# A transformer layer's step order: attention units, projections, modulation tiles and parts of the recurrence are named one by one, and some are moved

## The chip, the cores and the metric

The kernel runs on one core of a Trainium2 chip. The core has a matrix engine (TensorE, PE in the profile, with its weight loads as PEld), a vector engine (VectorE, DVE), a scalar engine (ScalarE, ACT), a general engine (GpSimd, POOL) and a queue processor that issues nearly all DMAs here (SyncE, SP). Each engine takes its instructions in one fixed order; semaphores tie them together. The metric is the device time of one execution in microseconds (us). Three runs of the kernel before took 1702.09, 1701.49 and 1700.19 us: the median is 1701.49 us.

## The reference

One layer of a streaming encoder, for 1024 prompt frames of one stream and 64 new frames of another (with a cache of 256 past frames), model width 1024, all in fp32:

```
mod = silu(c) @ w_ada + b_ada                 # 6 vectors: shift, scale, gate, twice
h   = rms_norm(x) * (1 + sc1) + sh1
proj = h @ w_in                               # one projection for both head groups
# 8 RWKV-7 heads of 64: r, k, v, decay, a, g from proj (token shift, small up-projections)
s = s*w - (s@kk)(kk*a) + v k ;  y = s @ r     # per frame, per head: 64 x 64 state
y = (group_norm(y) + bonus) * sigmoid(dg) @ w_gate_up
# 8 forgetting-attention heads of 64: QK-norm, cumulative log-forget bias, causal softmax
mix = concat(y_rwkv, y_fox) @ w_out
x = x + gt1 * mix
h2 = rms_norm(x) * (1 + sc2) + sh2
x = x + gt2 * ((silu(h2 @ w_gate) * (h2 @ w_up)) @ w_down)
```

Outputs are x, the recurrent states, the shift rows, and keys, values and log-forget values of the attention heads.

## The kernel before

**Matrix products.** fp32 accuracy is had from operands that are split in a high and a low part (`split`, L212 on ACT for the high part, L216 on DVE for the low one). `mm3` (L291 to L296) makes three matmuls for each block of 128 rows: high weights by high data (L294), high by low (L295), low by high (L296). A weight block of 128x1024 comes by DMA into the ring `wraw` (four buffers), its parts into `whi` and `wlo` (two buffers each).

**Stages.** The tokens are worked on in two halves: half 0 has 512 prompt frames, half 1 the other 512 and the 64 new ones. In the order of the trace: a start, in which the first 16 of 40 modulation tiles are made and `h` with them (to about 35 us); the phase of half 0 (to about 340 us) and of half 1 (to about 720 us), with the projections, the RWKV heads and the preparation of attention; attention of half 0 (about 665 to 744 us); attention of half 1 with the output projection of half 0 between its heads (about 744 to 905 us); output projection of half 1 and the second norm; the feed-forward part (to about 1430 us) and its down projection to the end.

**What sets the order.** The program emits steps one after another, and a list scheduler then orders the instructions of each engine. It works on the emission order with dependencies and buffers known, so neighbouring steps are interleaved, but a step that is emitted much later is not pulled far forward. Three things set the emission order:

- `ORDER` (L35, L36), a string of tokens for each half that `phase` reads. D, Z, A, B, N are an RWKV head pair's decay part, its three projections (k, r and v, with the square of k), its preparation, its chain over chunks of 64 frames, and its normalisation with the gate; T and U do a chain and a normalisation that half 0 left over; Q, K, q, k, V, C, L, O, S, P belong to attention's inputs, the log-forget values and the statistics.
- `proj` (L298): before it loads a projection's weights it takes one modulation tile off the list `background` and does it whole. There are 24 of these. Such a tile (`ada_mm`, L181 to L193, and `ada_fin`, L195 to L201) is a load `wada` into the ring `wraw`, 16 matmuls into `pada` with 32 columns of the array each, a copy `mrow` on ACT (L193), a transpose on PE (`pada<-ident,mrow`, L198) and a sum `mred` on DVE (L200).
- `Pipe(2)` in `run` (L1461, L1483). `attend` gives a head's units (two query blocks of 256 in half 0, three in half 1). A unit is a generator with stops: scores `psc` (L910, L912, mask L916), row maximum `nm` on DVE (L920), exponential `p` on ACT (L922) and scaling; then transposes `ppt` (L940) whose results are split to `pth` (ACT, L953) and `ptl` (DVE, L954); then `pav` (L962) and the output `fy` (DVE, L969). `Pipe` keeps two units under way and steps them in turn.

For half 1's attention the program calls `residual_x` (loads of x into `x1_0`, L996) and then `load_mix` of half 0 after head 0. `load_mix` brings eight blocks of mixed heads back from memory (`mixt<-yscr`, L984, two buffers): the first four are RWKV output (split to `mixrh`, `mixrl`), the others attention output that half 0's attention has stored from `fy` (L974, split to `mixfh`, `mixfl`). After each head but the first one tile of the output projection is done (`outproj`, result `po`, by `mm3`; its evacuation is on DVE, L1002). Since half 1's attention has other PSUM pools on the same banks, its first scores wait for the last `fy` of half 0.

Of the kernel before, what the change touches and what calls it, by code (L numbers as in the profile page):

```python
# [10 lines left out]
AF = mybir.ActivationFunctionType  # L11
# [5 lines left out]
P = 128  # L17
D = 1024
# [16 lines left out]
ORDER = ("Z0 D0 A0 D1 Z1 L Q0 B0 V0 N0 A1 C0 Z2 D2 q0 O A2 K0 k0 B1 K1 V2 Z3 D3 Q1 q1 V1 C1 A3 S k1 Q2 N1 q2 Q3 B2 N2 K2 k2 V3 K3 k3 C2 q3 C3",  # L35
         "Z0 T3 L D0 A0 Z1 U3 D1 B0 Q0 A1 D2 K0 Z2 A2 k0 D3 Q1 q0 N0 B1 K1 k1 q1 Z3 A3 N1 V0 V1 B2 V2 Q2 N2 q2 K3 Q3 q3 P B3 K2 k3 k2 V3")  # L36
# [28 lines left out]
class K:  # L65
# [351 lines left out]
    def rwkv_a(self, hf, j, z, d):  # L417

        nc, vc, O = self.nc, self.vc, self.O
# [4 lines left out]
        zk, zr, zv, sq = z  # L424
# [22 lines left out]
        for h in range(2):  # L447
# [6 lines left out]
            bon[:, off:off + m], ps, zv[:, off:off + m], op=ALU.mult), "ra")  # L454

        At = self.rpool.tile([P, 9, 2, 2, 64], F32, tag="At", name="At")
        for c in range(0, nch, 4):
            m = min(4, nch - c)

            pa = [self.ps([P, 4, P], tag="ra", name="pA") for _ in range(2)]  # L460
            for i in range(m):
                for h in range(2):
                    hp = slice(64 * h, 64 * h + 64)
                    nc.tensor.matmul(pa[h][:, i], kb[hp, c + i], rk[hp, c + i], start=True, stop=True)  # L464
            for h in range(2):
                nc.vector.tensor_tensor(At[:, c:c + m, :, h], pa[h][:, 0:m].rearrange("p i (x t) -> p i x t", x=2),
                                        self.amask[:, h:h + 1].rearrange("p o (x t) -> p o x t", x=2)
                                        .to_broadcast([P, m, 2, 64]), op=ALU.mult)

# [30 lines left out]
    def rwkv_b(self, hf, j, st):  # L500
# [14 lines left out]

        def small(name, blocks, mm):
# [20 lines left out]
        for h in range(2):  # L537
            for x in range(2):
                r = 64 * h + 32 * x
                nc.scalar.copy(inv[r:r + 16, 0:nch, r + 16:r + 32], pg[h][r:r + 16, 0:nch, 16:32])  # L540

# [16 lines left out]
        nc.gpsimd.memset(rk[64:128, 0:nch, 0:64], 0.0)  # L558

# [9 lines left out]
        for t0 in range(0, nch, 8):  # L569
# [6 lines left out]
            for x in range(min(2, m)):  # L576
                for h in range(2):
                    nc.scalar.copy(sv[64 - 64 * h:128 - 64 * h, t0 + x:t0 + m:2, h],
                                   pt[64 * x:64 * x + 64, 0:(m - x + 1) // 2, 64 * h:64 * h + 64])

# [8 lines left out]
        for c in range(nch):  # L589
            if c == 8:  # L590
# [385 lines left out]


# [310 lines left out]
    def phase(self, hf, order, late):  # L1288
# [13 lines left out]
        d, z, st, y, y0, f = {}, {}, {}, {}, {}, {}  # L1302
        for t in order:
            op, j = t[0], int(t[1]) if len(t) > 1 else 0
            if op == "D":
                d[j] = self.rwkv_d(hf, j, zl)
            elif op == "Z":
                zk = self.proj_z(hf, 4 + j)
                sq = self.slot(name="sq", tag="sa")
                nc.scalar.activation(sq[:, 0:hf.n], zk[:, 0:hf.n], AF.Square, scale=self.vc[:, V_KK + j:V_KK + j + 1])  # L1310
                z[j] = zk, self.proj_z(hf, j), self.proj_z(hf, 8 + j), sq
            elif op == "A":
                st[j] = self.rwkv_a(hf, j, z.pop(j), d.pop(j))
            elif op == "B":
                y[j] = self.rwkv_b(hf, j, st.pop(j))
            elif op == "N":
                self.rwkv_n(hf, j, y.pop(j), zg)
            elif op == "T":
                y0[j] = late[j][0]()
            elif op == "U":  # L1320
                late.pop(j)[1](y0.pop(j))
            elif op == "L":
                self.logf(hf)
            elif op == "O":
                self.ones_rows()
            elif op in "QK":
                f[t] = self.fox_qk(hf, j, int(op == "K"))
            elif op in "qk":
                self.fox_norm(hf, j, int(op == "k"), f.pop(t.upper()))
            elif op == "V":  # L1330
                self.fox_v(hf, j)
            elif op == "C":
                self.cache_kv(j)
            elif op == "P":
                self.early()
            elif op == "S":
                self.rs1 = self.x_stat1()
        r = {j: (lambda j=j, s=s: self.rwkv_b(hf, j, s), lambda p, j=j: self.rwkv_n(hf, j, p, zg)) for j, s in st.items()}
        for j, p in y.items():
            r[j] = (lambda p=p: p, lambda p, j=j: self.rwkv_n(hf, j, p, zg))  # L1340
        return r

    def run(self):
        tc, nc, A, O = self.tc, self.nc, self.A, self.O
        halves = [Half(0), Half(1)]
        with ExitStack() as top:
# [104 lines left out]
            for b, f in late.values():  # L1451
                f(b())
# [8 lines left out]
            pipe = Pipe(2)  # L1461
            for hd in range(8):
                pipe.run(self.attend(hd, halves[0]))
            pipe.flush()
# [18 lines left out]
            pipe = Pipe(2)  # L1483
            for hd in range(8):
# [8 lines left out]
            pipe.flush()  # L1493
            self.outproj(halves[0], 7)
# [114 lines left out]
class Pipe:  # L1609


    def __init__(self, skew):
        self.skew, self.live = skew, []

    def run(self, units):
        for u in units:
            self.live.insert(0, u)
            self.step(self.skew)

    def step(self, keep):  # L1620
        self.live = [u for u in self.live if next(u, None) is not None]
        while len(self.live) > keep:
            u = self.live.pop()
            for _ in u:
                pass

    def flush(self):
        while self.live:
            self.step(len(self.live))


# [91 lines left out]
```

## Time and profile before

| what | value |
|---|---|
| runs | 1702.09, 1701.49, 1700.19 us; median 1701.49 |
| the profiled execution's own time | 1699.15 us |
| its span, first to last instruction | 1697.5 us |
| busy in the span | PE 97%, PEld 85%, DVE 66%, ACT 43%, POOL 11% |
| mean granted clock of PE | 0.992 |

The difference between the profiled execution's time and its span, 1.65 us, lies around the instructions and no order changes it. The profiled execution was 2.34 us below the median of the runs. In the page's lines a name left of `<-` is what an instruction writes, those right of it what it reads; a bracket with a releaser gives the idle time of the engine just before the instruction and what ended it. In a table of windows the columns after the stretch are its length, then the busy time of PE, PEld, DVE, ACT and POOL with the number of instructions, the granted PE clock as a share of full speed, the share of the DMA engines and GB/s.

### The profile page before, as it was taken

Reading aid. Unit: us, or ns where it says so; the run is one execution under the profiler, and the core shown is the slowest. Engines: PE = TensorE matmul, PEld = TensorE weight load, DVE = VectorE, ACT = ScalarE, POOL = GpSimd, SP = SyncE. Lnnn points to the kernel's source line nnn. Section 1 sums busy time; section 2 is a strip of 40 time slices with the busy share of each in tenths; the row PEclk is TensorE's granted clock in tenths of the full one; section 3 lists DMA queues with packets and bytes.
Section 4 is the critical chain, followed back from the end, with each engine's and each line's share of the span. In section 5 each row is a group of like instructions: output and inputs, shape, how many; then the busy total and the mean of one; then the engine's idle time right before and its main releaser. Section 6 shows DMA issues by size and latency. Waiting matters only on the chain.

```text
span 1697.5 us, 33265 instructions
## 1 busy us (share of the span) xinstructions
PE 1645.3 (97%) x12897; PEld 1439.1 (85%) x12897; DVE 1124.8 (66%) x2573; ACT 726.5 (43%) x1530; POOL 183.1 (11%) x412
## 2 busy tenths in 40 slices
PE   6999999999999999989999999999999999999999
PEld 3776776788888888767889899999999999999998
DVE  6776676757867655877877975555555556545545
ACT  4535364653545346766776633333333333211210
POOL 2102230222121213201120000000000000000000
PEclk9999999999999999989999999999999999999999
DMA  8544447541233344566654432222222215323313
GB/s 308 164 128 133 141 135 200 176 123 33 71 85 85 87 135 113 149 190 179 169 181 167 157 127 77 77 77 77 77 77 77 77 65 196 134 79 97 97 40 121
DMA packets 133580, 207.08 MB, mean 122 GB/s; under 512 B 62126, under 2 KB 70350, under 8 KB 133422
## 3 DMA queue, kind: packets, MB, share of 16 engines
q1 hardware_dynamic: 133422, 204.95, 39.5%
q8 instruction: 102, 1.67, 0.4%
q14 instruction: 56, 0.46, 0.1%
HBM read 157.65 MB, written 47.25 MB: 121 GB/s over the span
## 4 chain that ended last, share of the span: by engine, by line
PE 84%; DVE 6%; ACT 4%; DMA 3%; issue 2%; SPq 0%; POOL 0%; ACTq 0%; DVEq 0%; POOLq 0%
PE pd L1275 15%; PE pfe L1160 8%; PE pfc L1160 7%; PE pfa L1160 7%; PE pmm L294 5%; PE pmm L295 5%; PE pmm L296 5%; PE pfb L1160 4%; PE pbs L375 2%; PE pav L962 2%; PE po L294 2%; PE ppt L940 2%; PE po L296 2%; PE po L295 2%; PE pA L464 2%
## 5 line engine op out<-in xcount | busy, mean ns | idle before, releaser
L294 PE MATMUL pmm<-hhi,whi 128*128 128x288 f32 (+1 forms) x624 | 218.8, 351 | 2.3 <-ACT pb L317 1.4
L295 PE MATMUL pmm<-hlo,whi 128*128 128x288 f32 (+1 forms) x624 | 217.0, 348 | 0.0
L296 PE MATMUL pmm<-hhi,wlo 128*128 128x288 f32 (+1 forms) x624 | 215.2, 345 | 0.6 <-DVE wlo L216 0.6
L212 ACT CAST whi<-wraw 128x1024 fp32r<-128x1024 f32 (+2 forms) x116 | 99.2, 855 | 212.5 <-PE pd L1275 167.0
L1275 PE MATMUL pd<-ah,wlo 128*128 128x512 f32 (+1 forms) x528 | 173.5, 329 | 0.0
L1275 PE MATMUL pd<-al,whi 128*128 128x512 f32 (+1 forms) x528 | 173.3, 328 | 0.0
L1275 PE MATMUL pd<-ah,whi 128*128 128x512 f32 (+1 forms) x528 | 173.1, 328 | 0.0
L1279 DVE SCALAR_TENSOR_TENSOR x1t<-pd,mod,x1t 128x512 f32<-128x512 f32 x192 | 91.4, 498 | 111.5 <-PE pd L1275 111.0
L294 PEld LDWEIGHTS pmm<-hhi,whi 128*128 128x128 f32 x624 | 119.0, 191 | 14.1 <-ACT pb L317 2.0
L296 PEld LDWEIGHTS pmm<-hhi,wlo 128*128 128x128 f32 x624 | 118.7, 190 | 10.9 <-issue 1.7
L295 PEld LDWEIGHTS pmm<-hlo,whi 128*128 128x128 f32 x624 | 118.7, 190 | 9.9 <-issue 1.2
L216 DVE TENSOR_TENSOR wlo<-wraw,whi 128x1024 fp32r<-128x1024 f32 (+2 forms) x108 | 104.2, 965 | 18.8 <-ACT whi L212 18.3
L1275 PEld LDWEIGHTS pd<-al,whi 128*128 128x128 f32 x528 | 99.4, 188 | 7.7
L1275 PEld LDWEIGHTS pd<-ah,whi 128*128 128x128 f32 x528 | 99.3, 188 | 7.7
L1275 PEld LDWEIGHTS pd<-ah,wlo 128*128 128x128 f32 x528 | 99.3, 188 | 7.5
L1160 PE MATMUL pfc<-hh,hS 128*128 128x256 f32 (+1 forms) x352 | 101.6, 289 | 1.6 <-ACT hh L1062 1.6
L1160 PE MATMUL pfc<-hl,hS 128*128 128x256 f32 (+1 forms) x352 | 101.9, 289 | 0.0
L1160 PE MATMUL pfa<-hh,whi 128*128 128x256 f32 (+1 forms) x352 | 101.9, 290 | 0.0
L1160 PE MATMUL pfa<-hl,whi 128*128 128x256 f32 (+1 forms) x352 | 101.8, 289 | 0.0
L1160 PE MATMUL pfc<-hh,lS 128*128 128x256 f32 (+1 forms) x352 | 101.5, 288 | 0.0
L1160 PE MATMUL pfa<-hh,wlo 128*128 128x256 f32 (+1 forms) x352 | 101.4, 289 | 0.0
L604 POOL TENSOR_SCALAR sd<-sv,pc 64x64 f32<-64x64 f32 x136 | 76.3, 561 | 181.2 <-DVE sv L617 157.6
(361 smaller groups left out, 4383.5 us busy)
## 6 DMA issues: line engine op xcount, KB each, us to landing
wraw<-in_w_in_dram SPq DMA_DIRECT2D x52, 512.0 KB
wada<-in_w_ada_dram SPq DMA_DIRECT2D x48, 512.0 KB
as<-actscr SPq DMA_DIRECT2D x22, 544.0 KB
wraw<-in_w_gate_dram SPq DMA_DIRECT2D x22, 512.0 KB
wraw<-in_w_up_dram SPq DMA_DIRECT2D x22, 512.0 KB
wraw<-in_w_down_dram SPq DMA_DIRECT2D x40, 256.0 KB
wraw<-in_w_out_dram SPq DMA_DIRECT2D x16, 512.0 KB
actscr<-sg SPq DMA_DIRECT2D x22, 288.0 KB
```

What stands on the lines that cost most here:

```text
L212: nc.scalar.copy(hi, src)
L216: eng.tensor_tensor(lo, src, hi.bitcast(F32), op=ALU.subtract)
L294: nc.tensor.matmul(ps[0:M, 0:n], whi[:, k, 0:M], xhi[:, k, off:off + n], start=(k == 0), stop=False)
L295: nc.tensor.matmul(ps[0:M, 0:n], whi[:, k, 0:M], xlo[:, k, off:off + n], start=False, stop=False)
L296: nc.tensor.matmul(ps[0:M, 0:n], wlo[:, k, 0:M], xhi[:, k, off:off + n], start=False, stop=(k == kt - 1))
L375: nc.tensor.matmul(ps[:, 0:n], w, x[:, off:off + n], start=True, stop=True)
L464: nc.tensor.matmul(pa[h][:, i], kb[hp, c + i], rk[hp, c + i], start=True, stop=True)
L604: nc.gpsimd.tensor_scalar(sd[hsl[h]], sv[hsl[h], c, h], pc[hsl[h], c], None, op0=ALU.mult)
L940: nc.tensor.transpose(pt[0:rows, b - b0, t * P:t * P + qn], p[0:qn, pc:pc + rows], self.ident[0:qn, 0:qn])
L1160: nc.tensor.matmul(ps, l[:, k], r[:, s, k], start=(first and k == 0 and y == 0), stop=(k == 3 and y == 2), skip_group_check=True)
L1275: nc.tensor.matmul(ps[:, 0:n], w[:, i], x[:, t:t + n], start=(i == 0 and y == 0), stop=(i == len(fs) - 1 and y == 2))
L1279: nc.vector.scalar_tensor_tensor(dst, ps[:, so - off:so - off + l], self.mod[:, 40 + o, b:b + 1], dst, op0=ALU.mult, op1=ALU.add)
```

## The change

The strings get finer tokens and some tokens stand elsewhere. Z is cut into X (k and its square), Y (r) and W (v). G does one modulation tile, which `proj` no longer does. A and B become generators, and a token with `*n` advances one by n stops. `Pipe` is gone; a table `ATT` tells for each half which unit advances at each step (a number advances that unit by one stop, H starts a head's loads, R is `residual_x`, M and N are `load_mix` of half 0 and half 1, O is one tile of the output projection). M is now the first token of half 1's attention, ahead of the first head's loads; R follows the first steps of units 0 and 1; O0 comes after unit 3's steps.

```diff
-ORDER = ("Z0 D0 A0 D1 Z1 L Q0 B0 V0 N0 A1 C0 Z2 D2 ...
+ORDER = ("W0 X0 G Y0 G D0 A0*2 G A0 D1 G X1 G Y1 G W1 L G Q0 B0*12 G V0 N0 A1*3 C0 G X2 ...
...
+       "M H0 0 1 0 R 2 1 0 H1 3 2 1 4 3 2 5 4 3 O0 H2 6 5 4 7 6 5 8 6 7 O1 H3 9 8 7 10 9 8 11 10 9 O2 H4 12 11 10 13 "
+       "14 12 11 13 12 O3 H5 15 14 13 16 15 14 17 16 15 O4 N H6 17 18 16 19 18 20 17 19 18 O5 H7 21 21 20 19 22 21 "
+       "20 23 O7 22 O6 23 22 23")
...
         else:
-            if self.background:
-                self.background.pop(0)()
             whi, wlo = self.load_w(self.A["w_in"][col // P], [P, KT, P])
...
+    def att_phase(self, hf, order, more):
+        units = {}
+        for t in order:
+            if t[0] == "H":
+                us = self.attend(int(t[1:]), hf)
+                units.update({int(t[1:]) * len(us) + i: u for i, u in enumerate(us)})
+            elif t.isdigit():
+                next(units[int(t)], None)
+            else:
+                more[t[0]](int(t[1:] or 0))
...
+                elif op == "G":
+                    self.background.pop(0)()
...
-            pipe = Pipe(2)
-            for hd in range(8):
-                pipe.run(self.attend(hd, halves[1]))
-                if hd == 0:
-                    self.residual_x(halves[0])
-                    self.load_mix(halves[0])
-                if hd:
-                    self.outproj(halves[0], hd - 1)
-                if hd == 5:
-                    self.load_mix(halves[1])
-            pipe.flush()
-            self.outproj(halves[0], 7)
+            self.att_phase(halves[1], ATT[1].split(), {
+                "R": lambda j: self.residual_x(halves[0]), "M": lambda j: self.load_mix(halves[0]),
+                "N": lambda j: self.load_mix(halves[1]), "O": lambda j: self.outproj(halves[0], j)})
```

The number and kind of instructions on each engine are the same. Their order differs in three places only: at the start of half 0's phase (about 34 to 125 us of the trace before), around the turn from half 0's attention to half 1's (about 725 to 800 us), and among the later heads of half 1 (about 800 to 955 us). The three pieces below are the ones that the prediction speaks of; line numbers in the rows of the change are those of the changed kernel, where `mm3` is at L306 to L308.

**SP, the DMA queue, at the turn.** Before, the loads of the mixed heads stand behind the stores and the residual's loads:

```order
L974 DMA yscr0_71<-fy_9046 128x512
L873 DMA q2x0_9558<-qx_73 4x576
L874 DMA k2x0_9560<-kx_74 4x1344
L876 DMA vsx0_9561<-vscr0_103 128x1280
L877 DMA vsx0_9561<-vscr0_103 64x128
L996 DMA x1_0_9536<-in_x0_dram 128x1024 x2
L974 DMA yscr0_71<-fy_9258 128x512
L996 DMA x1_0_9536<-in_x0_dram 128x1024 x2
L984 DMA mixt_9745<-yscr0_71 128x512
L984 DMA mixt_9749<-yscr0_71 128x512
```

With the change:

```order
L889 DMA k1x0_9559<-kx_74 64x1344
L1015 DMA mixt_9583<-yscr0_71 128x512
L1015 DMA mixt_9587<-yscr0_71 128x512
L665 DMA yscr1_72<-y_8242 128x576
L892 DMA q2x0_9558<-qx_73 64x576
L898 DMA vsx1_8034<-vscr7_110 128x512
L893 DMA k2x0_9560<-kx_74 64x1344
L993 DMA yscr0_71<-fy_9046 128x512
L1015 DMA mixt_9591<-yscr0_71 128x512
```

The first two mixed blocks are now asked for ahead of the store of `y`, thirteen rows earlier, and the next ones between the stores and the first head's loads.

**PE at the end of half 0's attention.** Here `pav_9491` is the last product of half 0 and `psc_9593` the first score of half 1. Before:

```order
L940 MATMUL ppt_9462<-ident_130,p_9434 128x128
L940 MATMUL ppt_9471<-ident_130,p_9434 128x128 x2
L962 MATMUL pav_9491<-pth_9463,vsx1_8034 128x256
L962 MATMUL pav_9491<-ptl_9464,vsx1_8034 128x256
...
L962 MATMUL pav_9491<-pth_9472,vsx1_8034 128x256
L962 MATMUL pav_9491<-ptl_9473,vsx1_8034 128x256
...
L910 MATMUL psc_9593<-k1x0_9559,qsx0_9557 128x512
```

With the change, from the last transposes on:

```order
L959 MATMUL ppt_9479<-ident_130,p_9434 128x128 x2
L307 MATMUL po_9983<-mixrl0_9544,whi_9979 128x512
L308 MATMUL po_9983<-mixrh0_9540,wlo_9980 128x512
L306 MATMUL po_9983<-mixrh0_9540,whi_9979 128x512
L981 MATMUL pav_9491<-pth_9471,vsx1_8034 128x256
L307 MATMUL po_9983<-mixrl0_9544,whi_9979 128x512
L308 MATMUL po_9983<-mixrh0_9540,wlo_9980 128x512
L981 MATMUL pav_9491<-ptl_9472,vsx1_8034 128x256
...
L306 MATMUL po_9983<-mixrh0_9540,whi_9979 128x512
L307 MATMUL po_9983<-mixrl0_9544,whi_9979 128x512
L308 MATMUL po_9983<-mixrh0_9540,wlo_9980 128x512
L929 MATMUL psc_9625<-k1x0_9559,qsx0_9557 128x512
```

Twelve matmuls of the first output tile, four blocks of the RWKV half of `mix`, now stand among the last products of half 0 and before the first score of half 1. On DVE and ACT their splits (four of `mixrh`, four of `mixrl`) move to the same place.

**PE near the start.** Before, a modulation tile and its transpose stand on both sides of a projection's matmuls:

```order
L402 MATMUL plora_955<-xl_776,wlo1_660 128x512
L190 MATMUL pada_1099<-wada_1097,ct_141 32x128 x8
L294 MATMUL pmm_1120<-hhi_175,whi_1116 128x512
L375 MATMUL pbs_975<-sq_840,bones_634 128x512
L295 MATMUL pmm_1120<-hlo_176,whi_1116 128x512
L296 MATMUL pmm_1120<-hhi_175,wlo_1117 128x512
L198 MATMUL pada_1099<-ident_130,mrow_1108 128x128
```

With the change, three of them meet between two projections:

```order
L202 MATMUL pada_920<-wada_918,ct_141 32x128 x8
L409 MATMUL plora_938<-xl_776,whi1_658 128x512
L412 MATMUL plora_937<-xl_776,wlo0_659 128x512
L412 MATMUL plora_938<-xl_776,wlo1_660 128x512
L202 MATMUL pada_1008<-wada_1006,ct_141 32x128
L210 MATMUL pada_920<-ident_130,mrow_929 128x128
L202 MATMUL pada_1008<-wada_1006,ct_141 32x128 x7
L210 MATMUL pada_1008<-ident_130,mrow_1017 128x128
L202 MATMUL pada_1098<-wada_1096,ct_141 32x128 x8
L210 MATMUL pada_1098<-ident_130,mrow_1107 128x128
L385 MATMUL pbs_958<-sq_861,bones_634 128x512
L306 MATMUL pmm_1120<-hhi_175,whi_1116 128x512
```

In return the projections ahead of it, W0 and X0, follow the ones made at the start with no modulation tile between them.

More of the change, by code (lines that the diff above doesn't have):

```diff
@@ L454, in rwkv_a @@
             bon[:, off:off + m], ps, zv[:, off:off + m], op=ALU.mult), "ra")
+        yield
         At = self.rpool.tile([P, 9, 2, 2, 64], F32, tag="At", name="At")
@@ L468, in rwkv_a @@
                                         .to_broadcast([P, m, 2, 64]), op=ALU.mult)
+        yield
         nb = 2 * ng
@@ L514, in rwkv_b @@
                 nc.sync.dma_start(inv[r, 0:nch, r], du[g, x].rearrange("g s t -> s g t"))
+        yield
         def small(name, blocks, mm):
@@ L558, in rwkv_b @@
         nc.gpsimd.memset(rk[64:128, 0:nch, 0:64], 0.0)
+        yield
         kbt = kb
@@ L579, in rwkv_b @@
                                    pt[64 * x:64 * x + 64, 0:(m - x + 1) // 2, 64 * h:64 * h + 64])
+        yield
         hsl = [slice(0, 64), slice(64, 128)]
@@ L589, in rwkv_b @@
         for c in range(nch):
+            if c:
+                yield
             if c == 8:
@@ L1301, in phase, with step @@
         self.sigm(zg[:, 0:hf.n], 1.0)
-        d, z, st, y, y0, f = {}, {}, {}, {}, {}, {}
+        d, z, f, gen = {}, {}, {}, {}
+        st, y = {}, {}
+        def step(key, make, done, j):
+            if key not in gen:
+                gen[key] = make()
+            try:
+                next(gen[key])
+            except StopIteration as e:
+                done[j] = e.value
+        y0 = {}
         for t in order:
+            t, _, times = t.partition("*")
             op, j = t[0], int(t[1]) if len(t) > 1 else 0
[L1305 to L1341, printed above, removed]
+            for _ in range(int(times or 1)):
+                if op == "D":
+                    d[j] = self.rwkv_d(hf, j, zl)
+                elif op == "X":
+                    zk = self.proj_z(hf, 4 + j)
+                    sq = self.slot(name="sq", tag="sa")
+                    nc.scalar.activation(sq[:, 0:hf.n], zk[:, 0:hf.n], AF.Square, scale=self.vc[:, V_KK + j:V_KK + j + 1])
+                    z[j, 0], z[j, 3] = zk, sq
+                elif op == "Y":
+                    z[j, 1] = self.proj_z(hf, j)
+                elif op == "W":
+                    z[j, 2] = self.proj_z(hf, 8 + j)
+                elif op == "G":
+                    self.background.pop(0)()
+                elif op == "A":
+                    step(t, lambda: self.rwkv_a(hf, j, [z.pop((j, i)) for i in range(4)], d.pop(j)), st, j)
+                elif op == "B":
+                    step(t, lambda: self.rwkv_b(hf, j, st.pop(j)), y, j)
+                elif op == "N":
+                    self.rwkv_n(hf, j, y.pop(j), zg)
+                elif op == "T":
+                    step(t, late[j][0], y0, j)
+                elif op == "U":
+                    late.pop(j)[1](y0.pop(j))
+                elif op == "L":
+                    self.logf(hf)
+                elif op == "O":
+                    self.ones_rows()
+                elif op in "QK":
+                    f[t] = self.fox_qk(hf, j, int(op == "K"))
+                elif op in "qk":
+                    self.fox_norm(hf, j, int(op == "k"), f.pop(t.upper()))
+                elif op == "V":
+                    self.fox_v(hf, j)
+                elif op == "C":
+                    self.cache_kv(j)
+                elif op == "P":
+                    self.early()
+                elif op == "S":
+                    self.rs1 = self.x_stat1()
@@ L1343, in run @@
+        return {j: (lambda j=j, s=s: self.rwkv_b(hf, j, s), lambda p, j=j: self.rwkv_n(hf, j, p, zg)) for j, s in st.items()} | {
+            j: (lambda: iter(()), lambda p, j=j: self.rwkv_n(hf, j, p, zg), p) for j, p in y.items()}
     def run(self):
@@ L1450, in run @@
             hst.close()
-            for b, f in late.values():
-                f(b())
+            for _, f, p in late.values():
+                f(p)
             nc.sync.dma_start(O["shift"], self.ns)
@@ L1460, in run @@
             self.att_pools(att, R)
-            pipe = Pipe(2)
-            for hd in range(8):
-                pipe.run(self.attend(hd, halves[0]))
-            pipe.flush()
+            self.att_phase(halves[0], ATT[0].split(), {})
             at0.close()
@@ L1606, in run @@
             self.down(halves, pre, x1t, lambda g, f: self.act_load(f, apools[g % 2]))
[L1609 to L1629, printed above, removed]
 class Rows:
```

12 lines of the change are left out of this document (7 added, 5 removed), and 1 row of the table ATT.

## The prediction

> **What bounds the kernel now.** I read the page's head first, then the chain of waits, then windows of the region that the change touches, and last PE's own timeline there.
>
> ```profile
> span 1697.5 us, 33265 instructions
> ...
> PE 1645.3 (97%) x12897; PEld 1439.1 (85%) x12897; DVE 1124.8 (66%) x2573; ACT 726.5 (43%) x1530; POOL 183.1 (11%) x412
> ...
> PE 84%; DVE 6%; ACT 4%; DMA 3%; issue 2%; SPq 0%; POOL 0%; ACTq 0%; DVEq 0%; POOLq 0%
> ```
>
> PE is the bound, with 97% of the span busy and 84% of the chain that ended last. No instruction is added or removed, so the change can only fill PE's holes, open new ones, or alter the clock at which PE's work runs. The whole of PE's idle time is 1697.5 - 1645.3 = 52.2 us, and that is spread over everything; the order is untouched outside three places. So the question is how much is lost there. The windows around the turn from half 0's attention to half 1's:
>
> ```profile
> 725.00:740.00 15.00, 11.39 (x66) 7.92 (x66) 13.44 (x38) 10.44 (x32) 1.71 (x11) 1.00 0.65 196
> 740.00:755.00 15.00, 12.92 (x45) 9.61 (x45) 7.89 (x15) 6.93 (x15) 0.41 (x2) 0.55 0.72 218
> 755.00:780.00 25.00, 22.77 (x121) 16.65 (x122) 19.75 (x39) 16.75 (x35) 3.01 (x5) 1.00 0.65 185
> 780.00:830.00 50.00, 49.22 (x307) 40.00 (x306) 39.90 (x85) 34.69 (x80) 5.85 (x14) 1.00 0.58 147
> 880.00:930.00 50.00, 50.00 (x338) 45.74 (x337) 37.79 (x64) 32.46 (x55) 2.14 (x5) 1.00 0.43 149
> ```
>
> Three things are to be seen. In the first stretch PE idles 3.61 of 15 us while DVE is busy 13.44: DVE sets the pace of half 0's last units. In the second PE looks busy (12.92), but the granted clock is 0.55: it works at half rate. In the third it idles 2.23 us at full clock. Later, from 780 us on, there is next to nothing left to fill (0.78 us, then 0.00). PE's idle time in the first three is 7.92 us together.
>
> PE's timeline tells which waits these are:
>
> ```profile
> 738.69 0.33 PE L940 MATMUL ppt<-ident,p 128*128 128x128 f32 x1 [1.02 <-DVE p L928]
> ...
> 741.12 0.39 PE L962 MATMUL pav<-pth,vsx 128*128 128x256 f32 x1 [0.46 <-ACT pth L953]
> 741.85 0.58 PE L962 MATMUL pav<-ptl,vsx 128*128 128x256 f32 x1 [0.34 <-DVE ptl L954]
> ...
> 744.68 0.80 PE L910 MATMUL psc<-k1x,qsx 128*128 128x512 f32 x1 [0.97 <-DVE fy L969]
> ```
>
> The last unit of half 0 goes from engine to engine with nothing beside it: transposes, split, product, evacuation, and only then half 1's first scores. 1.02 + 0.46 + 0.34 + 0.97 = 2.79 us are lost so.
>
> **Part 1: filler at the turn.** The first mixed blocks wait on SP in the order of the program, not for data:
>
> ```profile
> 730.19 0.94 SPq L874 DMA_DIRECT2D k2x<-kx  x1
> ...
> 744.66 0.33 SPq L974 DMA_DIRECT2D yscr<-fy  x1
> 745.03 0.92 SPq L996 DMA_DIRECT2D x<-in_x_dram  x2
> 746.00 0.90 SPq L984 DMA_DIRECT2D mixt<-yscr  x2
> ```
>
> The store `yscr<-fy` at 744.66 holds SP until half 0's last `fy`, and `mixt` stands behind it. With the change the first two `mixt` stand thirteen rows earlier, ahead of the store of `y`, so they go out before 730 us. One pair of their splits and the rate of the matmuls are in these rows (tile views of `mixrl` and `mixrh`, timeline of PE):
>
> ```profile
> L216 DVE TENSOR_TENSOR mixrl<-mixt,mixrh x4: 664/674/683, 756.5 to 763.0; 128x512 fp32r<-128x512 f32 x4
> ...
> L212 ACT CAST mixrh<-mixt x8: 616/648/675, 754.7 to 847.7; 128x512 fp32r<-128x512 f32 x4, 128x576 fp32r<-128x576 f32 x4
> ...
> 757.47 0.39 PE L295 MATMUL po<-mixrl,whi 128*128 128x512 f32 x1
> 757.70 0.39 PE L296 MATMUL po<-mixrh,wlo 128*128 128x512 f32 x1
> 757.93 0.39 PE L294 MATMUL po<-mixrh,whi 128*128 128x512 f32 x1
> ```
>
> A `po` follows the one before after 0.23 us, so twelve of them are 2.76 us of PE work that comes to stand in the 2.79 us of holes. Against it: four `mixrl` at 0.67 us are 2.7 us more on DVE, which in the first stretch has only 15 - 13.44 = 1.56 us free; three of them stand before half 0's last split. What is behind them on DVE is the `ptl` and `fy` for which PE waits. The bounds are a gain of 2.8 us (all filled, DVE's added work fits in its own waits) and a loss of 1 us (2.7 less 1.56, with the fillers waiting too). I take +1.5 us, since the last `fy` itself waited while DVE had nothing to do after 742.8 us.
>
> **Part 2: the half clock.** Windows of one stretch at a time:
>
> ```profile
> 742.00:755.00 13.00, 11.72 (x39) 8.84 (x39) 6.57 (x13) 5.70 (x12) 0.41 (x2) 0.50 0.74 213
> 755.00:756.00 1.00, 1.00 (x9) 1.00 (x9) 1.00 (x2) 1.00 (x3) 0.00 (x0) 0.97 0.37 91
> ...
> 738.20:741.60 3.40, 2.36 (x12) 1.53 (x12) 2.53 (x8) 2.15 (x6) 0.00 (x0) 0.97 0.72 276
> ...
> 277.00:278.00 1.00, 1.00 (x3) 0.80 (x4) 0.88 (x3) 0.26 (x1) 0.00 (x0) 0.59 0.80 262
> ...
> 280.00:281.00 1.00, 1.00 (x4) 0.64 (x3) 1.00 (x2) 0.04 (x1) 0.00 (x0) 0.70 0.98 272
> ```
>
> The clock falls right after a 3.4 us stretch in which PE was busy 2.36 us, and comes back at about 755. An earlier fall began at 277.4 and ended at 280.7 us (0.59 and 0.70 of a us at the mean say so). 11.72 us of PE work at half rate are 5.86 us at full rate, so 5.9 us is the most that can be won. With up to 2.76 us of dense matmuls in the stretch that brought the clock down, and the next fillers (`po<-mixfh`) between half 1's first scores, I expect that it mostly stays up. Bounds 0 and 5.9; I take 4.5 us, because an early return is worth most of it as well.
>
> [...]
>
> **Part 3: the rest of the turn.** At 766.90, 771.11 and 771.84 PE waited 0.68, 0.50 and 0.23 us:
>
> ```profile
> 766.90 0.30 PE L962 MATMUL pav<-pth,vsx 128*128 128x64 f32 x1 [0.68 <-DVE fy L969]
> ...
> 771.11 0.50 PE L294 MATMUL po<-mixfh,whi 128*128 128x512 f32 x1 [0.50 <-ACT mixfh L212]
> 771.84 0.50 PE L295 MATMUL po<-mixfl,whi 128*128 128x512 f32 x1 [0.23 <-DVE mixfl L216]
> ```
>
> The attention blocks of `mix` come too late for `po` because the `mixt` share two buffers and stand between the second head's loads on SP. With the change all eight stand ahead of the second head's loads. Bounds 0 and the 2.23 us of the stretch; I take 1.2 us. In the later heads (780 us and on) nothing can be won, and heads 3 and 4 lose their filler between scores; with PE idle 0.00 to 0.78 us in 50 I take 0, with bounds of 2 us lost and 1 us won.
>
> **Part 4: modulation tiles near the start.** Here the change opens holes. The nearest rows:
>
> ```profile
> 32.06 0.47 PE L198 MATMUL pada<-ident,mrow 128*128 128x128 f32 x1 [1.13 <-ACT mrow L193]
> ...
> 48.15 0.65 PE L190 MATMUL pada<-wada,ct 128*32 128x128 f32 x16
> 49.15 0.50 PE L294 MATMUL pmm<-hhi,whi 128*128 128x512 f32 x1 [0.36 <-ACT pb L317]
> ...
> 68.40 0.63 PE L402 MATMUL plora<-xl,wlo 128*128 128x512 f32 x2
> ...
> 66.00:71.00 5.00, 5.00 (x35) 3.37 (x34) 2.16 (x4) 2.34 (x5) 0.18 (x1) 1.00 0.44 127
> ```
>
> When a transpose directly follows its tile, PE waits 1.13 us for the copy `mrow`. Before, projections cover this (5.00 of 5 us busy at 66 to 71). With the change three tiles and their transposes meet at about 66 us. The first has three `plora` and one `pada` as cover, about 1 us, and costs 0.2; the second and third have none and cost 1.13 each: 2.5 us. In return the hole of 0.36 at 49.15 goes, since there is no `pada` tile to take the free PSUM buffer. If the clock falls after this thin stretch for as long as from 277.4 to 280.7 us, 3.3 us at half rate cost 1.7 more. Everything behind is PE-bound in unchanged order, so most of it lasts to the end, but some is taken up where PE waits for DVE later. Bounds: 0.4 won and 5 lost; I take 2.0 us lost.
>
> **The sum.** 1.5 + 4.5 + 1.2 + 0 - 2.0 = 5.2 us won. From the profiled execution's 1699.15 us this gives 1693.95; the runs' median was 2.34 us above that execution, so the forecast on their scale is 1696.3 us. About 0.2%, 3.4 us, can be told from no change: faster means below 1698.1, slower above 1704.9.
>
> **The rivals.**
>
> *The clock stays up and the new holes near the start are covered.* For it: ACT has 2.34 us of work in 5 at 66 to 71, so `mrow` may be faster than at the start. Against it: the copy's way is serial, and DVE's splits are squeezed in where DVE is full. Gain 2.8 + 5.9 + 1.2 = 9.9 us, less 0.4: 1692.0 us.
>
> *The half clock persists.* The fall needs only one thin stretch, and half 0's last units stay bound by DVE, on which 2.7 us of splits are put. For it: the clock stayed low for 13 us although PE was busy 11.72 of them. Then part 2 is 0, and 1.5 + 1.2 - 2.0 = 0.7 us are won: 1700.8 us, no change.
>
> *The tiles near the start bring the clock down.* This is the slower side. Place: the three transposes at about 66 us. The stretch holds 2.5 us of idle time and matmuls of 32 columns, thinner than the stretch that brought the clock down at 741.6 (1.04 us idle in 3.4). If the clock falls and stays low twice as long as at 277.4 us (6.6 us at half rate, 3.3 lost), the price is 2.5 + 3.3 - 0.4 = 5.4 us, and if the turn gains nothing since `po` at the head of PE's queue waits for `mixrl` on the full DVE (part 1 at -1, part 2 at 0, part 3 at 1.2), 0.2 are won there, and the result is 1701.5 + 5.2 = 1706.7 us. It decides from about 3.4 us of net loss on.
>
> *The change does little.* If the twelve `po` find their blocks no earlier than before, parts 1 to 3 vanish, and part 4 alone leaves 1703.5 us, which counts as no change. The order of SP speaks against it: its first two `mixt` read RWKV blocks of half 0, whose phase ended near 340 us.
>
> **How the numbers follow.** Forecast (1694 to 1699) 0.42; clock up and start covered (1690 to 1694) 0.20; half clock persists or the change does little (1699 to 1704) 0.26; slower side 0.12. The forecast's case falls below 1698.1 nearly always (0.40 of 0.42), so faster is 0.61, the same 0.27, slower 0.12. The forecast's own range is 1694 to 1699; eight in ten need the neighbours: 1689 to 1703 leaves out a tenth on the slower side and the best of the fast case.
>
> **What would show it.** Part 1: `mixt` issued before 730 us, twelve `po` between the last `pav` of half 0, and holes under 1 us together there; wrong if PE waits at a `po` for `mixrl`, or if the last `fy` of half 0 comes later than 744.2 by more than the fillers' 2.8 us. Part 2: granted clock 1.00 through the 15 us after half 0's end; wrong if it is 0.5 again for more than 3.4 us. Part 3: no wait for `mixfh` or `mixfl`. Part 4: two or three idle times of about 1.1 us before `pada<-ident,mrow` near 66 to 71 us, and perhaps a low clock after. The forecast is wrong as a whole if the heads from 780 us on are slower by more than 2 us, or if the gain at the turn is given back in waits for loads of the second head, which now stand behind eight `mixt`.

## The result and the profile after

The changed kernel is slower. Its twelve runs have a median of 1705.54 us (1701.31 to 1712.54), against 1700.84 us (1697.81 to 1702.09) for twelve of the kernel before: a ratio of 1.0038, 95% interval 1.0028 to 1.0049. By this ratio that is about 6.5 us more (4.7 us by the medians), where 5.2 us less were forecast and the range ended at 1703.0. The profiled execution took 1703.73 us, 4.6 us more than the one before; it is among the changed kernel's quicker ones.

The head of the page after, with its span, the busy times and the chain that ended last:

```profile
span 1702.0 us, 33261 instructions
...
PE 1643.2 (97%) x12897; PEld 1436.8 (84%) x12897; DVE 1124.9 (66%) x2573; ACT 727.3 (43%) x1530; POOL 186.2 (11%) x412
...
PE 85%; DVE 5%; ACT 4%; DMA 4%; issue 1%; SPq 0%; POOL 0%; ACTq 0%; DVEq 0%; POOLq 0%
```

PE was busy 2.1 us less than before and the span is 4.5 us longer, so PE's idle time rose from 52.2 to 58.8 us. Where it rose, the windows of the changed kernel tell (columns as before):

```profile
725.00:740.00 15.00, 11.34 (x67) 7.92 (x65) 13.01 (x36) 11.73 (x35) 1.72 (x11) 1.00 0.65 187
740.00:755.00 15.00, 13.80 (x71) 10.12 (x72) 12.26 (x26) 10.37 (x24) 0.41 (x2) 1.00 0.73 241
755.00:780.00 25.00, 21.93 (x121) 16.41 (x120) 15.40 (x32) 13.39 (x28) 3.07 (x5) 1.00 0.89 207
780.00:830.00 50.00, 44.44 (x272) 35.28 (x271) 39.49 (x81) 34.02 (x77) 5.70 (x12) 0.97 0.50 129
880.00:930.00 50.00, 50.00 (x328) 44.43 (x328) 36.62 (x66) 31.80 (x60) 4.71 (x8) 1.00 0.48 162
```

Two things are to be seen. At the turn the half clock is gone: 1.00 from 740 to 755 us, where it was 0.55, with PE 13.80 us busy at full rate. From 780 to 830 us, where before PE was busy 49.22 of 50 us, it is busy 44.44. So the idle time does not grow at the turn but in the heads after it.

A place that both traces have in common dates it. These are rows of SP's timeline, the last store of `y` in half 1's phase and the first load of the feed-forward part's weights, in the kernel before:

```profile
729.80 0.35 SPq L646 DMA_DIRECT2D yscr<-y  x1
...
915.86 0.33 SPq L282 DMA_DIRECT2D wraw<-in_w_gate_dram  x1
```

and in the changed kernel:

```profile
731.12 0.32 SPq L665 DMA_DIRECT2D yscr<-y  x1
...
920.18 0.33 SPq L294 DMA_DIRECT2D wraw<-in_w_gate_dram  x1
```

The changed kernel comes to the turn 1.3 us late and leaves the attentions 4.3 us late. The 1.3 us do not come from the moved steps near the start. Behind these the changed kernel is still 0.9 us early, as the load of cached values shows, before and with the change:

```profile
346.67 0.52 SPq L830 DMA_DIRECT2D vcc<-in_cache_v_dram  x1
```

```profile
345.75 0.53 SPq L849 DMA_DIRECT2D vcc<-in_cache_v_dram  x1
```

Between there and the turn its profile has 6.8 us at half clock (from 382 us), which the profile before does not have at that place.

### The profile page after: what moved, and what is told of

Same layout as the page of the kernel before. It is cut to its first block, busy times and chain, and to the rows that moved or that the text cites. A ratio compares the mean times of both kernels' runs of the same rounds, so it can differ in the third digit from the quotient of the medians.

```text
span 1702.0 us, 33261 instructions
## 1 busy us (share of the span) xinstructions
PE 1643.2 (97%) x12897; PEld 1436.8 (84%) x12897; DVE 1124.9 (66%) x2573; ACT 727.3 (43%) x1530; POOL 186.2 (11%) x412
## 4 chain that ended last, share of the span: by engine, by line
PE 85%; DVE 5%; ACT 4%; DMA 4%; issue 1%; SPq 0%; POOL 0%; ACTq 0%; DVEq 0%; POOLq 0%
PE pd L1306 15%; PE pfc L1191 8%; PE pfe L1191 8%; PE pfa L1191 8%; PE pmm L306 5%; PE pmm L307 5%; PE pmm L308 5%; PE pfb L1191 4%; PE pbs L385 2%; PE pav L981 2%; PE po L306 2%; PE po L308 2%; PE po L307 2%; PE pA L475 2%; DMA wada<-in_w_ada_dram 2%; PE ppt L959 2%
## 5 line engine op out<-in xcount | busy, mean ns | idle before, releaser
L306 PE MATMUL pmm<-hhi,whi 128*128 128x288 f32 (+1 forms) x624 | 219.4, 352 | 1.3 <-ACT hhi L283 0.7
L308 PE MATMUL pmm<-hhi,wlo 128*128 128x288 f32 (+1 forms) x624 | 215.2, 345 | 0.6 <-DVE wlo L228 0.6
L306 PEld LDWEIGHTS pmm<-hhi,whi 128*128 128x128 f32 x624 | 119.3, 191 | 13.1 <-issue 1.3
L307 PEld LDWEIGHTS pmm<-hlo,whi 128*128 128x128 f32 x624 | 119.2, 191 | 10.8 <-DVE hlo L284 1.4
L308 PEld LDWEIGHTS pmm<-hhi,wlo 128*128 128x128 f32 x624 | 119.1, 191 | 10.7 <-issue 1.4
```

The source lines that it names most:

```text
L306: nc.tensor.matmul(ps[0:M, 0:n], whi[:, k, 0:M], xhi[:, k, off:off + n], start=(k == 0), stop=False)
L307: nc.tensor.matmul(ps[0:M, 0:n], whi[:, k, 0:M], xlo[:, k, off:off + n], start=False, stop=False)
L308: nc.tensor.matmul(ps[0:M, 0:n], wlo[:, k, 0:M], xhi[:, k, off:off + n], start=False, stop=(k == kt - 1))
```

## What happens between 780 and 831 us

Output tiles (`po`) are the work that PE has beside the softmax of half 1's heads. In the changed kernel's timeline of PE, the last matmul of the third tile and the first of the fourth are these rows, with the two longest of the waits between them:

```profile
796.81 0.40 PE L308 MATMUL po<-mixfh,wlo 128*128 128x512 f32 x1
...
798.61 0.50 PE L929 MATMUL psc<-k1x,qsx 128*128 128x512 f32 x1 [0.97 <-ACT p L941]
...
824.73 0.39 PE L981 MATMUL pav<-ptl,vsx 128*128 128x256 f32 x1 [1.87 <-DVE ptl L973]
...
831.08 0.50 PE L306 MATMUL po<-mixrh,whi 128*128 128x512 f32 x1
```

For 34 us there is no output tile at all. In the kernel before the same gap lies between 818.49 and 826.14 us:

```profile
818.49 0.48 PE L296 MATMUL po<-mixfh,wlo 128*128 128x512 f32 x1
826.14 0.48 PE L294 MATMUL po<-mixrh,whi 128*128 128x512 f32 x1
```

The weights of the first three tiles are in the ring long before (on SP at rows 338, 343 and 350 in the changed kernel). They were asked for between 603 and 628 us. As soon as `mix` is there, the scheduler puts all three wherever PE has room. Those of the fourth tile are asked for, and split, at the old place. SP and ACT before:

```profile
811.74 0.58 SPq L282 DMA_DIRECT2D wraw<-in_w_out_dram  x1
...
819.29 1.05 ACT L212 CAST whi<-wraw 128x1024 fp32r<-128x1024 f32 x1
```

and with the change:

```profile
813.07 0.58 SPq L294 DMA_DIRECT2D wraw<-in_w_out_dram  x1
...
820.48 1.03 ACT L224 CAST whi<-wraw 128x1024 fp32r<-128x1024 f32 x1
```

So the change lets the filler start some 16 us earlier without bringing its supply forward. It is used up by 797 us, and the heads from there to 831 us run bare and wait for DVE and ACT. The last part of the gap is not the load's: the low part of the fourth tile's weights, made on POOL, is ready at about 824.0 us, and the tile's first matmul at 831.08 us waits for nothing, so that its place in PE's fixed order sets those 7 us. I call this theory T1; the others on record are T2 (the loss comes from the phases), T3 (the early loads delay the second head's loads) and T4 (the order of the units, or the old attention as such, is what counts).

## The experiments

Every string of the kernel before can be written in the new tokens; a kernel so written has the same instructions in the same order on every engine as the kernel before. The experiments start from there or from the changed kernel. Each ratio is to the kernel before on the same chip, with its 95% interval.

**1. Only the phases.** The edit: `ORDER` as changed, `ATT` as before.

```diff
-       "M H0 0 1 0 R 2 1 0 H1 3 2 1 4 3 2 5 4 3 O0 H2 6 5 4 7 6 5 8 6 7 O1 ...
+       "H0 0 1 0 2 1 0 R M H1 3 2 1 4 3 2 5 4 3 O0 H2 6 5 4 7 6 5 8 7 6 O1 ...
```

> Changed step order in the two phases, the old order of both attentions (the old pairs of units, mixed heads loaded after head 0, one output tile after each head). Theory T1 (the three output tiles whose weights are on chip are used up too early, the fourth tile's weights come at their old place, and PE idles about 7 us near 797 to 831 us): the loss sits in attention, so this run is like before, ratio 0.999 to 1.001, and PE between 780 and 830 us is busy about 49 us. Theory T2 (the loss comes from the phases: the three modulation tiles near 66 us and a half-clock stretch near 383 us): this run keeps the loss, ratio 1.002 to 1.004. Theory T3 (the early loads of the mixed heads delay the second head's loads): like T1 here.

Measured: 0.9987 (0.9976 to 0.9998), median 1699.24 us. The phases' order is a small gain, and the interval just leaves out no change. PE from 780 to 830 us is busy 48.73 us. T2 falls. The medians differ by 1.4 us, the ratio says 2.2.

**2. Only the attentions.** `ORDER` as before, `ATT` as changed.

```diff
-ORDER = ("W0 X0 G Y0 G D0 A0*2 G A0 D1 G X1 ...
+ORDER = ("G X0 G Y0 G W0 D0 A0*3 D1 G X1 ...
```

> The old step order in the two phases (no modulation tiles put together), the changed order of both attentions. T1: the loss is kept, ratio 1.002 to 1.004, with PE busy about 44 of 50 us from 780 to 830 us. T2: the loss goes, ratio 0.997 to 1.001. T3: kept as with T1, but the idle time is at the second head (about 760 to 770 us), waiting for DMA, and not at 797 to 831.

Measured: 1.0036 (1.0025 to 1.0048). The whole loss is here. From 800 to 830 us PE idles 3.92 us as in the changed kernel (3.96). The place that T3 forecast for the idle time does not hold: PE waits 1.0 us for a DMA at the turn here, and in the next run for none.

**3. One token.** The kernel before with `M` moved.

```diff
-       "H0 0 1 0 2 1 0 R M H1 3 2 1 ...
+       "M H0 0 1 0 2 1 0 R H1 3 2 1 ...
```

> The kernel before with one edit: the mixed heads of half 0 are loaded ahead of half 1's first head instead of after it. T1: this single move is enough, ratio 1.002 to 1.004; output tiles 0 to 2 end near 797 us and the fourth begins near 825. T2: no loss, ratio 0.997 to 1.001, since the turn gains. T3: ratio 1.001 to 1.004 with DMA waits at the second head.

Measured: 1.0046 (1.0030 to 1.0061). This one move costs as much as the whole change; nothing else in the attentions' order is needed for it. Its windows around the hole, and one right behind it:

```profile
780.00:800.00 20.00, 18.92 (x113) 14.91 (x112) 15.75 (x33) 12.73 (x31) 0.70 (x4) 1.00 0.48 125
800.00:830.00 30.00, 25.46 (x155) 19.98 (x155) 23.69 (x49) 20.93 (x47) 4.87 (x8) 0.94 0.52 132
...
826.00:836.00 10.00, 10.00 (x36) 7.58 (x35) 5.90 (x11) 4.09 (x9) 0.41 (x2) 0.51 0.24 77
```

Of 30 us from 800 on PE idles 4.54, and then it works at half rate for 10 us more (0.51). In this profile the hole has a tail, the low clock behind it.

**4. Tiles one head earlier.** As 3, with every output tile but the last emitted one head earlier, which brings the fourth tile's load eight rows of SP forward.

```diff
-       ... O0 H2 6 5 4 7 6 5 8 7 6 O1 H3 ...
+       ... 2 1 0 R O0 H1 3 2 1 4 3 2 5 4 3 O1 H2 6 5 4 7 6 5 8 7 6 O2 H3 ...
```

> As the run before it (mixed heads first), and each output tile is emitted one head earlier, so that the weights of the fourth tile are asked for at least six rows of SP earlier. T1: the hole between the third and the fourth tile shrinks from about 22 to 10 us of PE work, and the gain of the turn stays: ratio 0.996 to 0.999. T2: same as the run before it. T3: no better than the run before it, ratio 1.001 to 1.004.

Measured: 1.0018 (1.0009 to 1.0026). Better than 3, not better than the kernel before. The idle time from 800 to 830 us is 2.69 us instead of 4.54, so the hole shrinks as T1 has it; from 860 to 900 us it is 1.37 us, much as in 3 (1.47). The gain that T1 forecast (0.996 to 0.999) did not come; T3's range held the number, but not its statement that the run is no better than 3.

**5. The fourth tile's weights alone.** The changed kernel, with the weights of tiles 0 to 3 asked for together ahead of half 1's attention (token `w`); on SP the fourth load moves from row 495 to 421.

```diff
-       "M H0 0 1 0 R ...
+       "M w0 w1 w2 w3 H0 0 1 0 R ...
```

> The changed kernel with one edit: the weights of the first four output tiles are asked for together, ahead of half 1's attention (on SP the fourth load moves from row 495 to about 421); the steps keep their order. T1 (PE starves because the fourth tile's weights come late): the idle time of about 5.6 us between 780 and 830 us goes, and a smaller one comes between the fourth and the fifth tile (near 830 to 850 us): ratio to the kernel before 0.998 to 1.002. T4 (the loss is in the order of the units themselves, not in the filler): the same as the changed kernel, 1.003 to 1.005.

Measured: 1.0067 (1.0052 to 1.0082), against the forecast of 0.998 to 1.002. Both theories missed the number; T1's place is right, its size wrong. The profiled execution took 1714.75 us, 4.8 us more than the median of the six. The windows from 780 us on:

```profile
780.00:800.00 20.00, 20.00 (x117) 15.64 (x116) 16.42 (x32) 12.46 (x29) 3.03 (x5) 1.00 0.38 99
800.00:830.00 30.00, 29.17 (x176) 24.12 (x176) 23.11 (x48) 20.50 (x45) 2.74 (x8) 0.94 0.56 147
830.00:860.00 30.00, 27.26 (x157) 21.64 (x158) 24.99 (x53) 22.46 (x52) 5.64 (x9) 0.94 0.48 136
860.00:900.00 40.00, 37.71 (x212) 30.23 (x211) 29.64 (x56) 24.62 (x52) 9.87 (x12) 0.91 0.64 200
```

The hole is filled where it was (0.83 us instead of 3.96 from 800 to 830) and comes back whole one tile later: from 780 to 900 us PE idles 5.86 us, in the changed kernel 5.73. The turn got worse as well (10.8 us idle from 725 to 780, against 7.9), with a wait of 2.33 us for the attention blocks of `mix`:

```profile
758.95 0.80 PE L298 MATMUL po<-mixfh,whi 128*128 128x512 f32 x1 [2.33 <-ACT mixfh L216]
```

**6. All weights early.** As 5, with tiles 4 to 7 each asked for one head earlier too.

```diff
+       ... O1 w4 H3 ... O2 w5 H4 ... O3 w6 H5 ... O4 w7 N H6 ...
```

> As the run before it, and the weights of tiles 4 to 7 are each asked for one head earlier too. T1: no hole is left in half 1's attention, PE is busy 49 of 50 us in each stretch from 780 to 930 us, and what the turn gained stays: ratio 0.995 to 0.999. T4: the same as the changed kernel, 1.003 to 1.005.

Measured: 1.0014 (1.0002 to 1.0025), median 1701.01 us. This takes back most of the change's loss. The profiled execution is the fastest of twelve, 1695.97 us, 5.0 us below their median, so its windows show the run at its best:

```profile
780.00:800.00 20.00, 20.00 (x121) 16.11 (x121) 15.62 (x32) 13.61 (x30) 3.12 (x5) 1.00 0.45 118
800.00:830.00 30.00, 29.48 (x187) 23.85 (x186) 23.77 (x50) 21.15 (x51) 4.87 (x8) 1.00 0.60 155
830.00:860.00 30.00, 29.98 (x181) 24.00 (x182) 24.20 (x53) 21.58 (x49) 5.28 (x10) 1.00 0.69 185
860.00:900.00 40.00, 39.19 (x238) 31.59 (x237) 30.64 (x63) 27.63 (x62) 5.32 (x10) 1.00 0.53 179
```

No hole is left from 780 to 900 us (1.35 us together, 5.73 in the changed kernel) and the clock stays at 1.00. With the supply of filler brought forward the loss of the heads goes in this profile, and most of the time with it: that is T1's core, and T4's statement for this run (1.003 to 1.005) falls. T1's forecast of a net gain (0.995 to 0.999) falls too. The idle time at the turn is 9.2 us now; from 725 to 755 us it is 7.28 us, where the changed kernel has 4.86.

**7. Mixed heads later.** The kernel before with `M` moved the other way.

```diff
-       "H0 0 1 0 2 1 0 R M H1 3 2 1 ...
+       "H0 0 1 0 R 2 1 0 H1 M 3 2 1 ...
```

> The kernel before with the loads of the mixed heads moved the other way: behind the loads of head 1 instead of ahead of them, the residual's loads earlier. T1: the first tile's matmuls start about 9 us later, and the tiles are spread more evenly, so the holes at the turn grow by up to 2 us and the later ones shrink by 1: ratio 0.999 to 1.002. T4: no statement.

Measured: 1.0045 (1.0031 to 1.0059), more than forecast. The turn idles 10.7 us from 725 to 780 (before: 7.9), and 1.63 us from 860 to 900 are followed, from 882 us on, by 10.2 us at half clock. The place of `M` in the kernel before is better than both neighbours tried.

**8. Weights early, mixed heads as before.** The edit of 6 on the kernel before.

> The kernel before with the weights of the output tiles asked for earlier, as in the run with all weights early, and the mixed heads loaded at their old place. T1: before this PE had only 0.8 us of idle time from 780 to 830 us, so there is nothing to win: ratio 0.999 to 1.001. T4 and a theory that the weights' time alone is worth something: faster, 0.996 to 0.998.

Measured: 1.0026 (1.0014 to 1.0038), where T1 expected no change and T4 a gain. The early loads alone do harm. From 780 to 900 us there is nothing to see (0.79 us idle); the turn idles 9.3 us instead of 7.9 and has two stretches at half clock (the mean clock is 0.89 from 725 to 755 us and 0.86 from 755 to 780). Why asking for weights earlier hurts the turn was not settled.

**9. The modulation tiles taken apart.** As 1, with the two G tokens around the first preparation moved to the end of half 0's phase.

```diff
-ORDER = ("W0 X0 G Y0 G D0 A0*2 G A0 D1 ... K3 k3 "
-         "C2 q3 C3",
+ORDER = ("W0 X0 G Y0 D0 A0*3 D1 ... K3 k3 "
+         "G G C2 q3 C3",
```

> The changed phases with the old attentions, as in the first run of this study, and with the two modulation tiles beside the first preparation moved to the end of half 0's phase, so that no three transposes meet near 66 us. The prediction priced that meeting at 2.5 us and more; the first run's trace showed 0.87 us of idle time there. If the trace is right: ratio to the kernel before 0.997 to 1.000, at most 1 us better than the first run (0.9987). If the prediction's price was right: 2 to 4 us better, 0.995 to 0.997.

Measured: 1.0107 (1.0086 to 1.0127), far off both forecasts and, with number 10, the slowest of all. The modulation tiles are filler as well, and moving two of them re-orders the phase behind them. PE from 440 to 560 us, in this run and then in the kernel before, and a part of it in this run:

```profile
440.00:560.00 120.00, 113.65 (x1119) 97.40 (x1117) 80.46 (x209) 56.85 (x132) 24.43 (x49) 0.93 0.31 75
...
458.00:474.00 16.00, 16.00 (x247) 14.38 (x248) 4.69 (x11) 5.77 (x13) 3.39 (x7) 0.50 0.07 12
```

```profile
440.00:560.00 120.00, 115.88 (x1187) 99.36 (x1187) 86.04 (x226) 59.88 (x142) 28.30 (x61) 1.00 0.34 81
```

2.2 us more idle time and 16 us at half clock, about 8 us of lost work, far away from the edit. These are about 10 of the 18 us by which the run is slower; the rest was not followed. As a measure of what the meeting of the three tiles costs this run is of no use, since it changed much more.

**10 and 11. Mixed heads between.** `M` after the first step of unit 0, all weights early, the units in the old order; 10 with the phases of 9, 11 with the changed phases.

```diff
+       "H0 w0 w1 w2 w3 0 M 1 0 2 1 0 R H1 3 2 1 ...
```

> The phases of the run before it; in half 1's attention the mixed heads are loaded after the first step of unit 0, behind half 0's end, and all output weights are asked for early. T1 (holes between output tiles and the stretches at half clock behind them set the loss): no hole over 1 us from 780 to 930 us, fillers at the turn from about 750 us on, ratio 0.995 to 0.999. T4 (the old attentions are best as they are): 1.001 to 1.004.

> The attention of the run before it with the changed phases as they are (three modulation tiles together). T1: within 0.1% of the run before it, 0.996 to 1.000. If the place of the two modulation tiles matters by more than their 0.87 us, the two runs differ by more than 0.2%.

Measured: 1.0113 (1.0085 to 1.0141) and 1.0003 (0.9990 to 1.0015); number 10 missed both forecasts, and the two were to be within 0.1% of each other. They differ by what 9 did to the phases. Number 11 is level with the kernel before: with the filler supplied and the mixed heads not too early, the changed kernel's loss is gone, and no gain is left over. Number 1 has the same phases and the old attentions, so the earlier mixed heads and weights won nothing. Of all kernels only number 1 was faster than the kernel before, by 0.13% (0.02 to 0.24%).

## Why the prediction was wrong

**What bounds the kernel** held: PE is busy 97% in both, and most of the difference is holes of PE and its clock.

**Part 1, filler at the turn (+1.5 us forecast): about half of it, 0.8 us.** The twelve `po` stand where the order put them, and the first `mixt` went out at 726.28 us, as forecast. PE's idle time from 725 to 755 us fell from 5.69 to 4.86 us, but from 755 to 780, the place of part 3, it rose from 2.23 to 3.07: 7.92 us together before, 7.93 after. The four holes of the last unit are gone, and others have come. These are four of the new ones in the changed kernel:

```profile
740.46 0.50 PE L306 MATMUL po<-mixrh,whi 128*128 128x512 f32 x1 [1.08 <-ACT p L941]
...
749.30 0.50 PE L307 MATMUL po<-mixfl,whi 128*128 128x512 f32 x1 [0.52 <-DVE mixfl L228]
...
758.88 0.50 PE L306 MATMUL po<-mixrh,whi 128*128 128x512 f32 x1 [0.66 <-DVE x L1033]
765.36 0.73 PE L929 MATMUL psc<-k1x,qsx 128*128 128x512 f32 x2 [1.69 <-DMA k1x<-kx]
```

The last one is the prediction's own warning, the second head's loads behind eight `mixt` (1.69 us). It is what T3 has of this profile; runs 2 and 3 lose as much without this wait.

**Part 2, the half clock (+4.5 us): right in this profile, not shown beyond it.** The low stretch from 741.6 to 755 us is gone from the profile, and 11.72 us of PE work at half rate were 5.9 us. But run 2, with the same attentions, has two stretches of 3.4 us at the turn:

```profile
731.00:735.00 4.00, 3.84 (x17) 3.28 (x18) 3.53 (x13) 2.87 (x8) 0.20 (x1) 0.57 0.57 172
758.00:762.00 4.00, 3.70 (x14) 2.77 (x14) 3.01 (x9) 3.69 (x8) 1.95 (x1) 0.60 1.02 219
```

And the mean granted clock over whole executions did not rise: it is 0.992 over the twelve of the changed kernel and 0.993 over the 25 of the kernel before that were timed beside run 1. The profiled execution has the highest clock of the twelve, 0.995. So the 5.9 us are in part the luck of two profiles, and the half clock is not bound to the turn: it comes in other places too (below). That a thin stretch brings the clock down was the author's reading of the one fall at 741.6 us and is not shown as the cause: in the changed kernel the clock also fell at about 383 us, with PE idle 0.07 us in the 6 us ahead.

**Part 3 (+1.2 us): wrong in sign, -0.8 us.** In this profile the wait for `mixfh` is gone, that for `mixfl` is 0.52 us, and the second head's loads came later, so that the stretch idles 0.8 us more. In runs 2, 3 and 5, with the mixed heads as early, PE waits 1.5, 1.6 and 2.33 us for `mixfh`.

**The step that failed** is the term for the later heads: "heads 3 and 4 lose their filler between scores; with PE idle 0.00 to 0.78 us in 50 I take 0, with bounds of 2 us lost and 1 us won". It names the loss of filler and then puts it at nothing, from a PE that was full there because tiles lay ready as filler. The forecast counted the filler moved to the turn as won and did not ask what the heads from 797 us on would then run beside. The profiles show 4.8 us more idle time from 780 to 830 us (5.56 instead of 0.78) and 3.4 us at half clock behind it (1.7 us), 6.5 us together; the prediction's own sign of being wrong as a whole, heads slower by more than 2 us, came true. Row 495 of SP for the fourth tile's weights stands unmoved while `mixt` goes thirteen rows up; the order shows that without any run.

With 5.9 us won at the turn and 6.5 lost here the sum would be a loss of 0.6 us, but the common rows show 3.0 us between 730 and 916 us. Idle time and clock do not tell all: matmuls also follow each other at longer distances within "busy": in the changed kernel the `po` at 831.08 us is followed by the next after 0.33 us, that one by the third after 0.24, with no wait between them. If each matmul is counted at the usual distance of its form in these traces (an estimate), PE does about 6.3 us more work in the changed kernel from 735 to 797 us, 8.0 us less from 797 to 831, and about 1 us less from there to 915, which is close to the 3.0 us. Counted so, run 2 wins 6.1 us at the turn in spite of its half clock, and run 3 wins 3.9. So there was a gain at the turn, in this profile near the 7.2 us that parts 1 to 3 forecast, and the heads took more than that back.

**Part 4, the tiles near the start (-2.0 us): the loss did not come.** The three transposes stand together as forecast, but cost 0.43 and 0.44 us, not 1.13 each:

```profile
67.46 0.33 PE L210 MATMUL pada<-ident,mrow 128*128 128x128 f32 x1
...
68.79 0.33 PE L210 MATMUL pada<-ident,mrow 128*128 128x128 f32 x1 [0.43 <-ACT mrow L205]
...
70.13 0.33 PE L210 MATMUL pada<-ident,mrow 128*128 128x128 f32 x1 [0.44 <-ACT mrow L205]
```

The price was taken from the start, where ACT has other work ahead of `mrow` (a 0.72 us `hhi` at 31.13 us); here ACT is free and the copy takes 0.27 us. The changed kernel is 0.9 us early behind these steps, in profiles of which the one before has 6.8 us at half clock near 31 us and the one after none. The run with the phases alone was 0.13% faster, about 2 us won where 2 were forecast lost; how much of that comes from the start was not separated.

**The rivals.** The slower side came near the right number (1706.7 us) by luck: it put the thin stretch near the start and DVE's splits at the turn. What it described, a thin stretch and a low clock with it, is what the profile shows, but at 797 to 831 us (PE idle 5.56 of 34 us, and 3.4 us at half clock from 826 us). Both conditions of the first rival, the clock up at the turn and little lost near the start, held for the most part in the profile, and its 1692.0 us is the farthest off: it had the same term of 0 for the later heads.

## What the runs showed of the hardware that was not expected

The low clock comes in steps. From windows of one microsecond, the stretches at half clock, each as the sum of twice what the granted clock lacks to 1 (pieces of up to 2.8 us at the very end of the spans are left out):

| kernel | stretches at half clock: start in us (length in us) |
|---|---|
| before | 31 (6.8), 277 (3.4), 673 (3.4), 741 (13.7) |
| changed | 276 (3.4), 382 (6.8), 826 (3.4), 979 (3.4) |
| 1, phases only | 22 (10.2), 275 (3.4), 381 (6.8), 746 (6.8), 975 (3.4) |
| 3, one token | 34 (3.4), 276 (3.4), 757 (6.8), 826 (10.2), 983 (3.4) |
| 6, all weights early | 25 (6.8), 383 (3.4), 766 (3.4) |
| 9, tiles taken apart | 30 (6.8), 109 (3.4), 177 (3.4), 378 (3.4), 457 (17.1), 679 (3.4), 764 (6.8), 788 (6.8), 996 (3.4) |

Every stretch listed is 3.4 us long, or two to five times that to within 0.1 us (6.8, 10.2, 13.7 and 17.1 us). A hole ahead of it does not explain every fall. The clock fell at about 383 us in the changed kernel with no hole ahead of it:

```profile
380.00:382.00 2.00, 2.00 (x20) 2.00 (x19) 0.62 (x4) 1.50 (x4) 0.00 (x0) 1.00 0.07 9
382.00:384.00 2.00, 2.00 (x13) 2.00 (x13) 1.57 (x5) 1.26 (x3) 0.00 (x0) 0.64 0.05 12
```

PE was busy there but for 0.07 us in the 6 us ahead of the fall, in part with matmuls of 8 columns (`plc`, 128x8, from 379.94 us on). And in run 3 the clock stayed at 0.51 from 826 to 836 us with PE busy 10.00 of 10 us. So PE's busy time as the profile has it tells neither this fall nor how long the clock stayed low in run 3; what sets them is not shown.

Where a stretch falls differs between profiles of nearly the same order: the one at 673 us before is missing in the others listed but for run 9, and the one near 383 is missing before and in run 3. A stretch of 3.4 us at the clock of 0.50 read inside such stretches (run 9, 458 to 474 us) is 1.7 us of PE work, so a single profile of this kernel carries a few microseconds of chance, and the profile of before, on which the forecast was built, had 13.7 us of half clock at the turn where the run with the phases alone, with the old attentions, had 6.8.

## What to carry to other kernels

Independent work that a scheduler can put into holes is a stock with its own supply: before moving its start forward, read from the order when the stock ends and where its next load stands, and carry the load and the stock forward together. Here that only took the loss back (runs 6 and 11) and won nothing. A stretch in which the bound engine has "nothing left to fill" is full because of that stock, and is the first place to look when the stock is spent elsewhere. Here a hole cost its length, and in some profiles a piece at half rate stood behind it (3.4 us in the changed kernel and 10.2 us in run 3, both from 826 us), so changes of a few microseconds are to be judged by many timed runs and by experiments that undo one part, not by one profile's share.
